# Scaling four PSUM banks behind the matmuls that fill their other halves, and keeping two SSM tables in their written order on VectorE

## The chip, the core and the metric

The kernel runs on one core of a Trainium2 chip. TensorE (PE in the profile, PEld its weight loads) multiplies and writes into eight PSUM banks of 128 partitions by 512 float32; VectorE (DVE), ScalarE (ACT) and GpSimd (POOL) do the element-wise work; the DMAs are all issued by SyncE's queue (SPq). The time is the device time of one execution in microseconds, and the number compared is the median of several executions.

## The reference, cut to what matters

One decoder layer on x of 512 tokens by 1024 features: a gated feed-forward network (FFN), a mixer of attention and a state space model (SSM), and a second FFN, each with an RMS norm ahead and behind.

```
h = x + 1/2 * post1(SwiGLU_1(pre1(x)))        # w_gate, w_up: 1024 x 2816, w_down: 2816 x 1024
u = pre_m(h);  [q | k | v | s] = u @ W_in
a = block-sparse causal attention(q, k, v);  z = GLU(S5 SSM over s)
h = h + post_m([rms(a) | rms(z)] @ W_out)
y = h + 1/2 * post2(SwiGLU_2(pre2(h)))
```

In the SSM every state decays by a complex factor a = exp(lam * dt). The kernel builds tables from lam, dt, b and c before the mixer needs them: the powers of one complex factor for 128 steps (the tiles `e0` and `e1`, real and imaginary part), and the input matrices (`si`, from the tiles `f` and `b`), besides two others. All are stored to DRAM and read again in the mixer.

## The kernel before, in words

All matrix products are done with operands split in two parts, a high one and a remainder (`w1`/`w2` of a weight, `xh`/`xl` or `sh`/`sl` of the activations), as three matmuls: high by high, high by remainder, remainder by high (L185, L186, L187). ScalarE makes the high parts, VectorE the remainders (L90/L91 and L274/L275 for weights, L463/L464 for the hidden rows).

**First FFN, start.** The input is transposed without its norm, since the norm of a token is one factor for a whole column. Four PSUM banks `gu_192` to `gu_195` hold gate and up products of the first two feature blocks; columns 0:256 are tokens 0 to 255, columns 256:512 the others. `first_half` fills the first halves with unnormalised activations. `halves` then fills the second halves, bank by bank, from activations that were normalised in time: 24 matmuls a bank. Behind the first of these banks comes `late_norm`: a matmul spreads the norms of tokens 0 to 255 over all partitions (L171), ScalarE copies the result into `rsb` (L173), VectorE and ScalarE scale and split the activations of these tokens (L177 to L179), and VectorE multiplies the first halves of the four banks by `rsb` (L181). Then feature blocks 2 to 7 follow in full width (banks `pg`, `pu`, 48 matmuls a block), and between their evacuations VectorE computes pieces of the SSM tables (`Tables.steps`, as many as `STEPS` says).

**First FFN, middle and end.** The feature blocks 8 to 21 are done in pairs with fewer products (L396), and then comes the down projection: 22 groups of 24 matmuls (L185 to L187, tile `d`), one for each block of the hidden rows, whose parts `sh` and `sl` sit in three rotating buffers. At each group one piece of `Tables.rest` is taken from a generator:

```
            for _ in range({0: 4, 1: 2}.get(i, 1)):
                next(self.filler or iter(()), None)
```

Its pieces are first eight steps of the powers (each a `cmul`, six VectorE instructions, L547 to L552, which doubles the powers known so far, at most 32 at once), then the eight stores of `e0` and `e1` (L721), then for each of four quarters the loads of `f` and `b` (L727, L728), one `cmul` into `st`, and two stores of `si` (L733). When eleven groups are done, `open_third` gives back the memory of the hidden rows of the second half and of the tables; the hidden parts and weights of the remaining eleven groups are put there, so these wait for the table's stores.

**What sets the order.** TensorE and GpSimd run in the order in which the program is written. On VectorE, ScalarE and SyncE a scheduler picks, at build time, from what its own timing holds ready; instructions under `high_priority` are picked first. Instructions wait for each other by tile regions and, in a PSUM bank, also where a matmul writes one half while another engine touches the other half. A marked instruction (`keep_in_program_order`) is kept behind the one written just before it on its engine.

Of the kernel before, what the change touches and what calls it, by code (L numbers as in the profile page):

```python
# [11 lines left out]
OP = mybir.AluOpType  # L12
# [3 lines left out]
P = 128  # L16
# [6 lines left out]
H = 256  # L23


class Core:
    def __init__(self, tc, ctx):
        self.tc = tc
        self.nc = nc = tc.nc
        self.ctx = ctx  # L30
        self.const = ctx.enter_context(tc.tile_pool(name="const", bufs=1))
        self.ps = ctx.enter_context(tc.tile_pool(name="ps", bufs=8, space=PSUM))
        self.wk = ctx.enter_context(tc.tile_pool(name="wk", bufs=1))
        self.wp = ctx.enter_context(tc.tile_pool(name="wp", bufs=4))
        self.identg = self.const.tile([P, P + NK], F32, name="ident")
        self.ident, self.gcol = self.identg[:, :P], self.identg[:, P:]
        self.h = [self.const.tile([P, D], F32, name=f"h{t}") for t in range(4)]
        self.xh = self.const.tile([P, NK, S], F32R, name="xh")
        self.xl = self.const.tile([P, NK, S], F32R, name="xl")
        self.mhalf = self.const.tile([P, 1], F32, name="mhalf")  # L40
        nc.vector.memset(self.mhalf, -0.5)
        self.n = 0
        self.xf = None
# [120 lines left out]
    def late_norm(self, banks):  # L164


        nc = self.nc
        v = nc.vector
        diag = self.diag
        pb = banks[-1][:, H:]  # L170
        nc.tensor.matmul(pb, nc.const_aps.tensor(1.0, [P, P], F32), diag[:, :H], start=True, stop=True)  # L171
        rsb = self.t512("rsb")[:, :H]
        nc.scalar.activation(rsb, pb, AF.Copy)  # L173
        for q in range(2):
            k = slice(4 * q, 4 * q + 4)
            f = self.xf[0][:, k]
            v.tensor_tensor(f, f, rsb.unsqueeze(1).to_broadcast([P, 4, H]), OP.mult)  # L177
            nc.scalar.activation(self.xh[:, k, :H], f, AF.Copy)
            v.tensor_tensor(self.xl[:, k, :H], f, self.xh[:, k, :H].bitcast(F32), OP.subtract)  # L179
        for b in banks:  # L180
            v.tensor_tensor(b[:, :H], b[:, :H], rsb, OP.mult)  # L181

    def mm3(self, out, ah, al, bh, bl, first, last):
        nc = self.nc
# [22 lines left out]
    def halves(self, units, hooks, begun=False):  # L207

        for half in range(begun, 2):
            for i, (u, pb) in enumerate(units):
                self.proj_T(u, pb, (half * H, half * H + H))
                if half == 0:
                    for f in hooks.get(i, ()):
                        f()
                if begun and i == 0:
                    with self.tc.high_priority(PRIO):
                        self.late_norm([pb for u, pb in units])

    def open_ffn(self, ctx, tab):

        def pool(name, c, bufs=1):
            self.n += 1
            return c.enter_context(self.tc.tile_pool(name=f"{name}_{self.n}", bufs=bufs, reuse_waits="tile"))
        self.hid = pool("hida", ctx)
        below, low, self.top = ExitStack(), ExitStack(), ExitStack()  # L230
        self.xsum = pool("xsum", below)
        self.filler = None
        if tab is not None:
            self.filler = tab.steps(pool("tab", self.top), self.nc.vector)

        def drain():
            for _ in self.filler or ():
                pass
            self.filler = None
            self.top.close()  # L240
            self.top = ExitStack()

        def first():
            drain()
            self.late = pool("hidb", low).tile([P, NF - HALF_F, S], F32, name=f"late_{self.n}")
            self.sum = pool("sum", self.top)

        def second():
            drain()
            p = pool("split", self.top, 3)  # L250
            if tab is not None:
                self.filler = tab.rest(pool("rest", self.top), self.xsum, self.nc.vector)
            return p

        def third():
            drain()
            low.close()
            below.close()
            return pool("last", self.top, LAST)
        self.open_first, self.open_second, self.open_third = first, second, third  # L260

    def ring(self, tag, n, dt):
# [263 lines left out]
PRIO = 400  # L526
# [18 lines left out]
def cmul(eng, ore, oim, ar, ai, br, bi, t1, t2):  # L545

    eng.tensor_tensor(t1, ar, br, OP.mult)  # L547
    eng.tensor_tensor(t2, ai, bi, OP.mult)
    eng.tensor_tensor(ore, t1, t2, OP.subtract)
    eng.tensor_tensor(t1, ar, bi, OP.mult)  # L550
    eng.tensor_tensor(t2, ai, br, OP.mult)
    eng.tensor_tensor(oim, t1, t2, OP.add)  # L552


class Tables:


# [140 lines left out]
    def rest(self, pool, wide, vec):  # L698


        nc, core = self.nc, self.core
        tt = wide.tile([P, 2, 512], F32, tag="t4", name="ett")
        tt = [tt[:, j] for j in range(2)]
        et = [wide.tile([P, 16, P], F32, tag=f"t{j + 1}", name=f"e{j}") for j in range(2)]
        vec.tensor_copy(et[0][:, :, 0], self.u4r)
        vec.tensor_copy(et[1][:, :, 0], self.u4i)
        n = 1
        while n < P:
            for lo in range(0, n, 32):
                m = min(32, n - lo)  # L710
                s1, s2 = (t[:, :16 * m].rearrange("p (c x) -> p c x", c=16) for t in tt)
                with core.tc.high_priority(PRIO):
                    cmul(vec, et[0][:, :, n + lo:n + lo + m], et[1][:, :, n + lo:n + lo + m],
                         et[0][:, :, lo:lo + m], et[1][:, :, lo:lo + m],
                         et[0][:, :, n - 1:n].to_broadcast([P, 16, m]), et[1][:, :, n - 1:n].to_broadcast([P, 16, m]),
                         s1, s2)
                yield
            n *= 2
        for q in range(4):
            for j in range(2):  # L720
                nc.sync.dma_start(self.e[j][q].rearrange("p (c x) -> p c x", c=4), et[j][:, 4 * q:4 * q + 4])  # L721
        for q in range(4):
            f, b = ([pool.tile([P, 512], F32, tag=f"{n}{j}", name=f"{n}{j}_{q}") for j in range(2)] for n in "fb")
            c = slice(512 * q, 512 * q + 512)
            for j in range(2):
                for s in range(4):
                    nc.sync.dma_start(f[j][32 * s:32 * s + 32], self.w[j, s:s + 1, c].partition_broadcast(32))  # L727
                nc.sync.dma_start(b[j], self.bturn[j, :, c])  # L728
            t = [pool.tile([P, 512], F32, tag=f"st{j}", name=f"st{j}_{q}") for j in range(2)]
            st = [core.t512("st") for j in range(2)]  # L730
            cmul(vec, *st, *f, *b, *t)
            for j in range(2):
                nc.sync.dma_start(self.si[j][q], st[j])  # L733
            yield
# [519 lines left out]
```

## Time and profile before

| | |
|---|---|
| median of 3 runs | 941.51 us (940.51 to 941.88) |
| profiled execution | 942.61 us, its span 940.6 us |
| mean granted TensorE clock | 0.989 of full speed |
| busy: PE, PEld, DVE, ACT | 98%, 88%, 73%, 45% of the span |
| TensorE waits of 1 us or more, each with its longest | gu on VectorE 5.4 us; sc on VectorE 2.4; d on ScalarE 2.4; d on VectorE 1.9 |

A row of the timeline has the start in microseconds from the span's start, the busy time, engine, line, operation, output and inputs with their shape, the count, and in brackets how long the engine was idle before and what ended that. A row of the windows has for each engine its busy time and instructions, then the granted TensorE clock (1.00 is 2.4 GHz, 0.50 is 1.2 GHz), the share of the DMA engines and their GB/s. In a row of waits stand the total, how often, and the longest.

### The profile page before, as it was taken

The page shows a single profiled execution, that of the slowest core. Times are in us where ns is not written, and L with a number is a line of the kernel's source. Part 1 is how long each engine was busy: PE and PEld are TensorE (multiplying, and loading weights), DVE is VectorE, ACT ScalarE, POOL GpSimd, SP SyncE. Part 2 cuts the span into 40 slices and gives each one's busy share as a digit, 9 for nine tenths or more (in the row PEclk, how much of TensorE's full clock was granted, in tenths as well). Part 3 has the DMA queues.
Part 4 walks back from the last instruction along what each step waited for, and adds up shares of the span by engine and source line. Part 5 has one row for each costly group of instructions (what it writes and reads, how often), then busy time and mean ns, then how long its engine had stood idle before and what let it go on. Part 6 is the DMA issues. An engine that isn't in the chain of part 4 may idle for free.

```text
span 940.6 us, 14870 instructions
## 1 busy us (share of the span) xinstructions
PE 918.6 (98%) x5815; PEld 824.7 (88%) x5815; DVE 689.0 (73%) x1179; ACT 427.8 (45%) x717; POOL 54.8 (6%) x47
## 2 busy tenths in 40 slices
PE   9799999999999899998999999999999999999997
PEld 8788899999988688987888778989999999988885
DVE  7997678888588655579999969698878887532623
ACT  7522345455422343333478866445445545422511
POOL 1400000000000001021120113000000000000000
PEclk9899999999999899999999999999999999999999
DMA  8436322322665561485432122322333323333302
GB/s 265 128 114 213 115 91 90 112 91 68 191 207 173 193 221 34 151 246 163 131 107 99 32 104 67 136 68 92 115 109 94 109 93 111 112 98 104 135 1 89
DMA packets 51574, 114.59 MB, mean 122 GB/s; under 512 B 9904, under 2 KB 20912, under 8 KB 51504
## 3 DMA queue, kind: packets, MB, share of 16 engines
q1 hardware_dynamic: 51504, 113.65, 37.5%
q8 instruction: 45, 0.74, 0.3%
q14 instruction: 25, 0.20, 0.1%
HBM read 102.62 MB, written 11.01 MB: 121 GB/s over the span
## 4 chain that ended last, share of the span: by engine, by line
PE 81%; DVE 8%; DMA 5%; ACT 2%; SPq 2%; issue 2%; POOL 0%; DVEq 0%; POOLq 0%; ACTq 0%
PE c L396 28%; PE d L187 6%; PE d L186 6%; PE d L185 6%; PE p L396 5%; DMA b<-in_bturn 2%; PE pg L185 2%; PE pg L187 2%; PE pu L187 2%; PE pu L185 2%; PE pg L186 2%; PE pu L186 2%; PE wo L187 1%; PE wo L185 1%; PE wo L186 1%
## 5 line engine op out<-in xcount | busy, mean ns | idle before, releaser
L396 PE MATMUL c<-xh,w 128*128 128x256 f32 x1024 | 187.2, 281 | 0.1
L396 PEld LDWEIGHTS c<-xh,w 128*128 128x128 f32 x1024 | 159.3, 189 | 0.3 <-DVE w L275 0.3
L90 ACT ACTIVATE w<-w 128x1024 fp32r<-128x1024 f32 x90 | 94.3, 1055 | 108.9 <-PE d L187 22.5
L396 PE MATMUL c<-xl,w 128*128 128x256 f32 x512 | 143.8, 281 | 0.0
L91 DVE TENSOR_TENSOR w<-w,w 128x1024 fp32r<-128x1024 f32 x90 | 111.3, 1243 | 41.2 <-ACT w L90 41.0
L185 PE MATMUL d<-w,sh 128*128 128x512 f32 x352 | 138.2, 393 | 2.4 <-ACT sh L463 2.4
L187 PE MATMUL d<-w,sl 128*128 128x512 f32 x352 | 138.1, 392 | 1.9 <-DVE sl L464 1.9
L275 DVE TENSOR_TENSOR w<-w,w 128x1024 fp32r<-128x1024 f32 x96 | 116.9, 1222 | 29.4 <-ACT w L274 28.8
L186 PE MATMUL d<-w,sh 128*128 128x512 f32 x352 | 137.9, 392 | 0.0
L274 ACT ACTIVATE w<-w 128x1024 fp32r<-128x1024 f32 x96 | 100.2, 1058 | 72.5 <-PE c L396 45.3
L396 PE MATMUL c<-t,w 128*128 128x256 f32 x768 | 97.4, 283 | 0.1
L396 PEld LDWEIGHTS c<-xl,w 128*128 128x128 f32 x512 | 96.6, 189 | 0.0
L396 PEld LDWEIGHTS c<-t,w 128*128 128x128 f32 x768 | 94.3, 191 | 0.3 <-DVE w L275 0.3
L185 PEld LDWEIGHTS d<-w,sh 128*128 128x128 f32 x352 | 66.7, 189 | 16.7 <-ACT sh L463 2.8
L187 PEld LDWEIGHTS d<-w,sl 128*128 128x128 f32 x352 | 66.7, 190 | 16.2 <-DVE sl L464 2.3
L186 PEld LDWEIGHTS d<-w,sh 128*128 128x128 f32 x352 | 66.7, 189 | 13.7
L61 POOL TENSOR_TENSOR rs<-v,mhalf 128x1 f32<-128x1 f32 x24 | 20.0, 835 | 733.6 <-DVE v L57 733.6
L396 PE MATMUL p<-t,s1h 128*128 128x256 f32 x256 | 46.5, 282 | 0.0
L463 ACT ACTIVATE sh<-late 128x512 fp32r<-128x512 f32 x22 | 13.4, 630 | 60.9 <-PE d L186 60.9
L456 ACT ACTIVATE sg<-c 128x256 f32<-128x256 f32 x64 | 24.5, 382 | 33.6 <-DVE c L414 26.8
L396 PEld LDWEIGHTS p<-t,s1h 128*128 128x128 f32 x256 | 39.7, 190 | 0.0
L396 PE MATMUL p<-t,s1l 128*128 128x256 f32 x128 | 36.1, 282 | 0.0
(318 smaller groups left out, 1768.8 us busy)
## 6 DMA issues: line engine op xcount, KB each, us to landing
w<-in_wgu SPq DMA_DIRECT2D x88, 512.0 KB, 3.6
w<-in_wd SPq DMA_DIRECT2D x44, 512.0 KB, 3.9
e<-e SPq DMA_DIRECT2D x16, 256.0 KB, 4.4
w<-in_wq SPq DMA_DIRECT2D x8, 512.0 KB, 3.8
g<-in_gains SPq DMA_DIRECT2D x5, 512.0 KB, 5.4
h<-in_x SPq DMA_DIRECT2D x4, 512.0 KB, 6.1
ca<-cx SPq DMA_DIRECT2D x8, 256.0 KB, 2.9
f<-win SPq DMA_DIRECT2D x32, 64.0 KB, 3.2
```

Of the source, the lines that this page charges most:

```text
L61: self.nc.gpsimd.tensor_tensor(rs, v, self.mhalf, OP.pow)
L90: nc.scalar.activation(hi, raw, AF.Copy)
L91: (eng or nc.vector).tensor_tensor(lo, raw, hi.bitcast(F32), OP.subtract)
L185: nc.tensor.matmul(out, ah, bh, start=first, stop=False)
L186: nc.tensor.matmul(out, ah, bl, start=False, stop=False)
L187: nc.tensor.matmul(out, al, bh, start=False, stop=last)
L274: nc.scalar.activation(hi, src, AF.Copy)
L275: nc.vector.tensor_tensor(lo, src, hi.bitcast(F32), OP.subtract)
L396: nc.tensor.matmul(out, l[:, s], r[:, kb + k, t], start=first and k == 0 and n == 0, stop=last and k == 3 and n == 2, skip_group_check=True)
L456: nc.scalar.activation(sg, pg, AF.Silu)
L463: nc.scalar.activation(hi, hidden[k], AF.Copy)
```

## The change

Two things are edited. The four multiplications of the banks leave `late_norm`; they are written behind the loop of `halves` and without high priority, so behind all second halves. And the powers lose their high priority; all VectorE instructions of `Tables.rest` (powers and inputs' table) now go through a small wrapper that keeps each behind the instruction written before it on VectorE. No operation is added or removed. (The rows of these instructions have the wrapper's line, L563, in the new kernel; other lines move down by 1 to 11.)

```
@@ late_norm
-        for b in banks:
-            v.tensor_tensor(b[:, :H], b[:, :H], rsb, OP.mult)
+        self.rsb = rsb
@@ halves
                 if begun and i == 0:
                     with self.tc.high_priority(PRIO):
                         self.late_norm([pb for u, pb in units])
+        for u, pb in units if begun else ():
+            self.nc.vector.tensor_tensor(pb[:, :H], pb[:, :H], self.rsb, OP.mult)
@@ open_ffn
-                self.filler = tab.rest(pool("rest", self.top), self.xsum, self.nc.vector)
+                self.filler = tab.rest(pool("rest", self.top), self.xsum, InOrder(self.tc, self.nc.vector))
+class InOrder:
+    def __init__(self, tc, eng):
+        self.tc, self.eng = tc, eng
+    def __getattr__(self, name):
+        return lambda *a, **k: self.tc.keep_in_program_order(getattr(self.eng, name)(*a, **k))
@@ rest
-                with core.tc.high_priority(PRIO):
-                    cmul(vec, ...)
+                cmul(vec, ...)
```

TensorE's and GpSimd's orders stay as they were. On the other engines rows move in three places.

**VectorE behind `late_norm`.** `gu` are the four banks, `xf` and `xl` the activations of tokens 0 to 255 and their remainders, `w_45` the weights of the second product of block 2. Before:

```order
L177 TENSOR_TENSOR xf_106<-xf_106,rsb_396 128x1024 x2
L181 TENSOR_TENSOR gu_192<-gu_192,rsb_396 128x256
L181 TENSOR_TENSOR gu_193<-gu_193,rsb_396 128x256
L181 TENSOR_TENSOR gu_194<-gu_194,rsb_396 128x256
L181 TENSOR_TENSOR gu_195<-gu_195,rsb_396 128x256
L604 SCALAR_TENSOR_TENSOR ssm_small<-ssm_small 128x16
L299 TENSOR_TENSOR xf_107<-xf_107,xf_106 128x1024
L582 TENSOR_TENSOR ssm_small<-ssm_small 128x16
L179 TENSOR_TENSOR xl<-xf_106,xh 128x4x256 x2
```

and now:

```order
L177 TENSOR_TENSOR xf_106<-xf_106,rsb_396 128x1024 x2
L220 TENSOR_TENSOR gu_192<-gu_192,rsb_396 128x256
L615 SCALAR_TENSOR_TENSOR ssm_small<-ssm_small 128x16
L220 TENSOR_TENSOR gu_193<-gu_193,rsb_396 128x256
L300 TENSOR_TENSOR xf_107<-xf_107,xf_106 128x1024
L593 TENSOR_TENSOR ssm_small<-ssm_small 128x16
L91 TENSOR_TENSOR w_45_572<-w_44_569,w_45_571 128x1024
L179 TENSOR_TENSOR xl<-xf_106,xh 128x4x256
L615 SCALAR_TENSOR_TENSOR ssm_small<-ssm_small 128x16
L220 TENSOR_TENSOR gu_194<-gu_194,rsb_396 128x256
L179 TENSOR_TENSOR xl<-xf_106,xh 128x4x256
```

The four scalings are spread, the last stands further down, behind what is shown, and a weight's remainder has come ahead of the two rows that make `xl`.

**VectorE near the end of the tables**, groups 8 to 11 of the down projection. `e_2848` and `e_2849` are the powers, `ett` their scratch, `st` the inputs' table. Before:

```order
L464 TENSOR_TENSOR sl_3319<-late_1031,sh_3318 128x512
L91 TENSOR_TENSOR w_327_3366<-w_326_3363,w_327_3365 128x1024
L549 TENSOR_TENSOR e_2848<-ett 128x16x32
L550 TENSOR_TENSOR ett<-e_2848,e_2849 128x512
L551 TENSOR_TENSOR ett<-e_2849,e_2848 128x512
L552 TENSOR_TENSOR e_2849<-ett 128x16x32
L91 TENSOR_TENSOR w_329_3400<-w_328_3397,w_329_3399 128x1024
```

and now:

```order
L563 TENSOR_TENSOR e_2848<-ett 128x16x32
L563 TENSOR_TENSOR st_3_3238<-f_3_3224,b_3_3226 128x512
L563 TENSOR_TENSOR ett<-e_2848,e_2849 128x512
L563 TENSOR_TENSOR ett<-e_2849,e_2848 128x512
L465 TENSOR_TENSOR sl_3319<-late_1031,sh_3318 128x512
L91 TENSOR_TENSOR w_327_3366<-w_326_3363,w_327_3365 128x1024
L563 TENSOR_TENSOR st_3_3239<-f_3_3225,b_3_3227 128x512
L563 TENSOR_TENSOR e_2849<-ett 128x16x32
L563 TENSOR_TENSOR st_3240<-st_3_3238,st_3_3239 128x512
```

The last write of `e_2848` has moved ahead of the remainders `sl_3319` and `w_327`, and the fourth quarter of the inputs' table, which stood ahead of it all before, is now partly behind the last write of `e_2849`.

**SyncE's queue at the same place.** `e_97` and `e_98` are the powers in DRAM, `w_330` and `w_332` raw weights. Before:

```order
L80 DMA w_330_3431<-in_wd 128x1024
L733 DMA si_94<-st_3241 128x512
L80 DMA w_332_3465<-in_wd 128x1024
L721 DMA e_97<-e_2848 128x512 x4
L721 DMA e_98<-e_2849 128x512 x4
L80 DMA w_334_3499<-in_wd 128x1024
```

and now:

```order
L80 DMA w_330_3431<-in_wd 128x1024
L730 DMA e_97<-e_2848 128x512 x4
L80 DMA w_332_3465<-in_wd 128x1024
L730 DMA e_98<-e_2849 128x512 x4
L742 DMA si_93<-st_3240 128x512
L80 DMA w_334_3499<-in_wd 128x1024
L742 DMA si_94<-st_3241 128x512
```

The first four stores of the powers have moved ahead of the load of `w_332`, and the last two stores of the inputs' table have moved behind the powers' stores.

More of the change, by code (lines that the diff above doesn't have):

```diff
@@ L711, in rest @@
                 s1, s2 = (t[:, :16 * m].rearrange("p (c x) -> p c x", c=16) for t in tt)
-                with core.tc.high_priority(PRIO):
[L713 to L716, printed above, removed]
+                cmul(vec, et[0][:, :, n + lo:n + lo + m], et[1][:, :, n + lo:n + lo + m],
+                     et[0][:, :, lo:lo + m], et[1][:, :, lo:lo + m],
+                     et[0][:, :, n - 1:n].to_broadcast([P, 16, m]), et[1][:, :, n - 1:n].to_broadcast([P, 16, m]), s1, s2)
                 yield
```

## The prediction

> **What bounds the kernel now.** I read first the busy times, then TensorE's waits, then the windows and the timeline around each wait. TensorE is busy 98% of the span, so only two things can shorten it: its waits, and stretches in which it runs at half clock.
>
> ```profile
> PE 918.6 (98%) x5815; PEld 824.7 (88%) x5815; DVE 689.0 (73%) x1179; ACT 427.8 (45%) x717; POOL 54.8 (6%) x47
> ```
>
> The list of TensorE's waits has four of a microsecond or more that the profile names once each:
>
> ```profile
> PE gu L185 <- DVE gu L181: 5.4, 1, 5.4
> PE sc L841 <- DVE y L942: 2.4, 1, 2.4
> PE d L185 <- ACT sh L463: 2.4, 1, 2.4
> PE d L187 <- DVE sl L464: 1.9, 1, 1.9
> ```
>
> The first stands in the stretch of the late scaling, the last two are one stop in the first down projection; the second belongs to the mixer, where the change moves nothing. The windows show that the first costs more than its wait:
>
> ```profile
> 27.00:32.30 5.30, 0.00 (x0) 0.00 (x0) 5.26 (x14) 2.12 (x4) 4.55 (x2) 0.69 0.36 120
> 32.30:36.00 3.70, 3.70 (x17) 3.70 (x18) 3.70 (x7) 3.19 (x4) 2.08 (x1) 0.52 0.79 256
> 36.00:40.00 4.00, 4.00 (x36) 4.00 (x35) 4.00 (x9) 1.45 (x2) 0.00 (x0) 1.00 0.02 4
> 112.00:200.00 88.00, 88.00 (x742) 88.00 (x741) 67.99 (x101) 43.51 (x71) 0.00 (x0) 1.00 0.30 99
> ```
>
> TensorE does nothing from 27.0 to 32.3, its clock falls to the lower level, 17 matmuls run at half speed, and only then is the clock full. In the 88 us of the pairs that follow it never stops while VectorE has 20 us to spare: what is won ahead of them is kept.
>
> **Term 1: the banks.** The timeline of TensorE (first four rows) and of VectorE around the wait:
>
> ```profile
> 26.25 0.70 PE L171 MATMUL gu<-diag,const-float32-1.0 128*128 128x256 f32 x2 [0.15 <-DVE diag L1218]
> 32.30 0.58 PE L185 MATMUL gu<-xh,first 128*128 128x256 f32 x1 [5.35 <-DVE gu L181]
> 36.12 0.28 PE L185 MATMUL gu<-xh,first 128*128 128x256 f32 x1
> 42.51 0.40 PE L185 MATMUL pg<-xh,w 128*128 128x512 f32 x1
> 29.22 2.35 DVE L177 TENSOR_TENSOR xf<-xf,rsb 128x1024 f32<-128x1024 f32 x2
> 31.49 1.42 DVE L181 TENSOR_TENSOR gu<-gu,rsb 128x256 f32<-128x256 f32 x4
> 32.91 1.23 DVE L299 TENSOR_TENSOR xf<-xf,xf 128x1024 f32<-128x1024 f32 x1
> 34.15 2.36 DVE L179 TENSOR_TENSOR xl<-xf,xh 128x1024 fp32r<-128x1024 f32 x2
> ```
>
> The matmul at 32.30 opens the second bank's second half, and waits until VectorE has scaled its first half, since that scaling was written ahead of it. Its operands were ready long before. In the change the 72 matmuls of banks two to four follow the norm matmul at once. That at 36.12 is the 19th, and the 54 from it to the first `pg` took 42.51 - 36.12 = 6.39 us, 0.118 each; so 72 take 8.52 us and `pg` could issue at 26.95 + 8.52 = 35.47 instead of 42.51: 7.04 us, of them 5.35 the wait and the rest the half clock.
>
> The next thing that can be late is `xl`, which the second `pg` matmul reads. In the new order VectorE does, from 31.49: two scalings (2 x 0.36), two small rows (0.2), L299 (1.23), a weight's remainder that has come ahead (1.22) and the first half of `xl` (1.18): 36.0 at most, 35.85 with the usual overlap of 0.1 a row. That matmul would issue at 35.7. I take 0.3 us of waiting; below it is 0, above it is 1.9, if the matmul waits for both halves of `xl` (one more scaling and 1.18 us, to 37.6). The short waits of 0.9 us at 9 us cost no clock, since the windows there are at 1.00:
>
> ```profile
> 0.00:10.00 10.00, 8.05 (x49) 6.21 (x49) 5.60 (x15) 6.29 (x12) 0.20 (x4) 1.00 0.80 295
> ```
>
> The scalings cost the same four times 0.36 us on VectorE. Now each waits for TensorE to leave its bank: the second bank at 26.95 + 2.84 = 29.8, the third at 32.6, the fourth at 35.5. VectorE reaches them at 31.9, 35.9 and about 40 (behind `xl`, a gain of 0.7, an evacuation of 0.7 and a weight of 1.2), so it waits for none. The Trainium skill speaks against cheap hopes here: "PSUM — Partial Sum Buffer", section "PSUM bank collisions raise a hardware error", says that two engines must not touch one bank at the same partitions at once, whichever columns; by it no scaling can run beside its bank's matmuls, and the sum is the same, as they are reached later anyway. The old 5.35 us between disjoint halves of a bank agree with it.
>
> What comes after on this side is the matmuls with table entries, which TensorE reaches 6.7 us earlier:
>
> ```profile
> 76.98 0.69 DVE L670 TENSOR_TENSOR cx<-tt,tt 128x512 f32<-128x512 f32 x1
> 87.30 0.27 PE L677 MATMUL si<-ident,win 128*128 128x128 f32 x1
> ```
>
> The third update of `cx` by L670 is the last these need; it ended at 77.7. In the new order two more weight remainders, two scalings and half of `xl` lie ahead of it and one weight less behind 36 us (2 x 1.22 + 0.72 + 1.18 - 1.22 = 3.1, less 0.6 that the queue starts earlier): 80.2 at most, against 80.6. Nothing, with 0.4 us to spare; the upper bound is 1 us. Behind them SyncE's queue has changed too:
>
> ```profile
> 80.75 5.50 SPq L694 DMA_DIRECT2D ca<-cx  x8
> 98.60 0.69 DVE L351 TENSOR_TENSOR h<-w 128x512 f32<-128x512 f32 x1 [1.08 <-DMA w<-in_wgu]
> 112.36 0.28 PE L396 MATMUL c<-xh,w 128*128 128x256 f32 x1
> ```
>
> The eight `ca` stores now leave behind the last `cx`, and the load that VectorE got at 98.6 waits for them. Even 7 us later, at 105.6, with two VectorE rows and one of ScalarE (2.0) on top, its sums are there at 107.6; TensorE wants them 36 matmuls of 0.118 into the pairs, at 112.36 + 4.2 - 6.7 = 109.9. No cost. Term 1 is 7.04 - 0.3 = **6.7 us**.
>
> **Term 2: the tables.** TensorE at the stop, the chain of waits (the row without a line number), and the two engines and the queue behind it:
>
> ```profile
> 304.79 0.39 PE L186 MATMUL d<-w,sh 128*128 128x512 f32 x1
> 311.82 0.39 PE L187 MATMUL d<-w,sl 128*128 128x512 f32 x1
> 314.61 0.50 PE L185 MATMUL d<-w,sh 128*128 128x512 f32 x1 [2.40 <-ACT sh L463]
> 317.23 0.79 PE L187 MATMUL d<-w,sl 128*128 128x512 f32 x1 [1.88 <-DVE sl L464]
> 322.79 0.39 PE L185 MATMUL d<-w,sh 128*128 128x512 f32 x1
> 313.93 0.63 ACT L463 ACTIVATE sh<-h 128x512 fp32r<-128x512 f32 x1 [6.06 <-DMA e<-e]
> 316.48 2.54 DVE L464 TENSOR_TENSOR sl<-h,sh 128x512 fp32r<-128x512 f32 x4 [4.83 <-DMA e<-e]
> 312.04 4.32 DMA e<-e
> 307.35 5.46 SPq L721 DMA_DIRECT2D e<-e  x8
> 308.68 0.69 DVE L552 TENSOR_TENSOR e<-ett 128x512 f32<-128x512 f32 x1
> 297.13 0.69 DVE L548 TENSOR_TENSOR st<-f,b 128x512 f32<-128x512 f32 x1 [3.00 <-DMA b<-in_bturn]
> ```
>
> The 32 matmuls from 304.79 to 311.82 are 0.227 apart. The one at 322.79 is the 16th of the twelfth group and would have come at 311.82 + 16 x 0.227 = 315.45: the stop costs 7.34 us, 4.28 waiting and 3.06 at half clock. Its cause: the memory of this group's parts holds the powers until all eight stores have left; these are issued in one row of 5.46 us from 307.35, the last at 312.04, which lands at 316.36.
>
> In the new order four rows of the inputs' table (the end of its fourth quarter, 4 x 0.69 = 2.8) stand behind the last write of the powers and no longer ahead of it. The wait of 3.00 for the load of `b` stood ahead too; the row that waits for that load now has a hidden row's remainder (0.69) and a weight's (1.22) and powers' rows ahead that used to be behind it. So the last write ends, in the time of before, at 309.37 - 2.8 = 306.6 at the latest, and at 309.37 - 2.8 - 3.0 = 303.6 if the load is covered, as I take it. The first four stores go out earlier, when `e0` is done, so four remain: three issues of 0.68 (5.46 / 8) and a landing of 4.32 after the last begins: 309.9, or 312.9 at the bound. The remainder then takes VectorE 0.69, and TensorE wants it at 312.05 + 0.45 = 312.5. At 309.9 there is no stop, 1.9 us to spare; at the bound it is 1.1 us late. So this term lies between 7.34 - 1.1 - 3.06 = 3.2 (late and clock lost) and 7.34; I take **7.3**, being nearer the first by the covered load. The remainders of groups 4 to 11 cost nothing either: adding up the rows of the new order, with the loads of `b` at the median below, each ends 2 to 6 us earlier than before against TensorE. The inputs' table is stored last at about 305, as before; the mixer's first load of it is at 380:
>
> ```profile
> b<-in_bturn SPq DMA_DIRECT2D x8, 256.0 KB, 4.5
> 304.89 0.69 DVE L464 TENSOR_TENSOR sl<-late,sh 128x512 fp32r<-128x512 f32 x1
> 380.30 0.80 SPq L893 DMA_DIRECT2D si<-si  x2
> ```
>
> **Sum.** 6.7 + 7.3 = 14.0 us. Against the profiled execution of 942.6 us this is 928.6; the median of the runs shown is 1.1 lower, so 927.5.
>
> **The rivals.**
> (A) Both stops go, as summed: 927.5.
> (B) The second stop stays in part: a load of `b` that lands late delays the last write. For it speaks the 3.00 us of before, against it that only one of six such waits was over 1.5 us:
>
> ```profile
> DVE st L548 <- DMA b<-in_bturn: 3.9, 2, 3.0
> DVE st L547 <- DMA b<-in_bturn: 3.6, 3, 1.5
> DVE st L548 <- DMA f<-win: 1.1, 1, 1.1
> ```
>
> Between 927.5 + 1.1 and, with the whole stop, 927.5 + 7.3: near 932.
> (C) The first stop turns into smaller ones, 1.6 more at `xl` or 1 at the table's matmuls, with up to 1.7 of half clock: 929 to 931.
> (D) Slower. VectorE works off its queue in order; with the table's rows held behind their predecessors, a row that waits for a load holds up the remainders behind it, as in those 3.0 us. TensorE notices once such waits together pass the lead of the remainders, some 6 us (that of group 11 was done at 305.6, can now be done near 303.6 - 0.69 - 0.69 - 1.22 = 301, and is used at 307). It decides once what is lost beyond that lead passes the 14.0 us of the sum; if the six rows wait 4 us longer each it is 24 us, 18 beyond the lead, and three stops with 3.06 of half clock each, so 27 us on top of 927.5: 954. Against it: those waits were 8.6 us in all. The Trainium skill has the rule in "PSUM — Partial Sum Buffer", section "Engine vs sequencer instructions": VectorE's queue is strictly first in, first out. By it a late load is paid in full by all that stands behind; the trace agrees with the 3.0 us.
> (E) The change does not do what it says: if TensorE also waited at 27 us for ScalarE or the activations, the stop would stay. The row of the wait names L181 alone. With the tables' stop kept as well, 941.5.
>
> **How the numbers follow.** A 70%, B 14%, C 9%, D 4%, E 3%. The range holds A with its unknown costs, C and the nearer part of B: from 925.5 (the 0.3 us at `xl` not paid and up to 1.7 of the mixer's 2.4 us gone) to 934.0. Faster by over 0.2%, which is about what a measurement of this kernel can tell from no change, are A, B and C: 0.93. Within it E: 0.03. Slower D: 0.04.
>
> **What would show it.** Right: no wait of `gu` for L220 at 27 us, windows from 27 to 40 at clock 1.00, `pg` at 35.5 to 36; the first `si` matmul near 80.6; no `d` wait for `sh` or `sl`, the last store of the powers issued before TensorE's group 11 ends, and clock 1.00 throughout the down projection. Wrong: a `pg` wait for `xl` of over 2 us, an `m` wait for `cx`, or `d` still waiting for the powers' stores, or for `sl` with VectorE held by a load of `b`.

## The result, and the profile after

The changed kernel takes 928.54 us (median of 4 runs, 927.66 to 929.68), the kernel before 941.69 us beside it (4 runs, 940.51 to 944.28). The ratio is 0.9843, with a 95% interval of 0.9822 to 0.9865; of 941.69 us that is 12.7 to 16.8 us saved. The two medians alone lie 13.15 us apart, inside that interval. In a second comparison the ratio was 0.9845 (0.9824 to 0.9866). The profiled execution took 929.68 us with a span of 927.9 (before 942.61 and 940.6). Forecast were 927.5 us and 14.0 saved.

The busy times, and three rows of the list of TensorE's waits, in the profile of the changed kernel:

```profile
PE 914.2 (99%) x5815; PEld 821.7 (89%) x5815; DVE 689.1 (74%) x1179; ACT 427.0 (46%) x717; POOL 54.9 (6%) x47
```

```profile
PE sc L850 <- DVE y L951: 2.6, 1, 2.6
PE gu L171 <- DVE diag L1227: 0.8, 1, 0.8
PE pg L185 <- DVE xl L179: 0.2, 1, 0.2
```

The wait of 5.4 us of `gu` for the scaled banks is gone, and so are both waits of `d` (2.4 and 1.9). The mixer's wait of `sc` stands as it stood. In place of the first wait there is one of 0.2 for `xl`. The windows of the two stretches (columns as in the prediction: window, its length, busy time of TensorE, weight loads, VectorE, ScalarE, GpSimd, then the granted clock, the DMA share and GB/s):

```profile
27.00:36.00 9.00, 8.76 (x72) 8.71 (x73) 8.96 (x19) 6.07 (x8) 6.96 (x3) 1.00 0.55 189
36.00:40.00 4.00, 3.79 (x18) 2.93 (x18) 4.00 (x8) 2.90 (x4) 0.00 (x0) 1.00 0.61 207
305.00:320.00 15.00, 15.00 (x67) 12.28 (x66) 10.44 (x13) 9.35 (x13) 0.00 (x0) 1.00 0.53 189
```

The stretch from 27 to 32.3 held no matmul before, and the one behind it ran at clock 0.52. Now TensorE works through, at 1.00. The timelines of TensorE and of VectorE there:

```profile
27.24 0.70 PE L171 MATMUL gu<-diag,const-float32-1.0 128*128 128x256 f32 x2 [0.79 <-DVE diag L1227]
27.58 0.47 PE L184 MATMUL gu<-xh,first 128*128 128x256 f32 x1
36.30 0.39 PE L184 MATMUL pg<-xh,w 128*128 128x512 f32 x1
36.89 0.50 PE L185 MATMUL pg<-xl,w 128*128 128x512 f32 x1 [0.21 <-DVE xl L179]
```

```profile
32.49 0.41 DVE L220 TENSOR_TENSOR gu<-gu,rsb 128x256 f32<-128x256 f32 x1
32.93 0.41 DVE L220 TENSOR_TENSOR gu<-gu,rsb 128x256 f32<-128x256 f32 x1
35.63 1.21 DVE L179 TENSOR_TENSOR xl<-xf,xh 128x1024 fp32r<-128x1024 f32 x1
36.88 0.41 DVE L220 TENSOR_TENSOR gu<-gu,rsb 128x256 f32<-128x256 f32 x1
40.76 0.41 DVE L220 TENSOR_TENSOR gu<-gu,rsb 128x256 f32<-128x256 f32 x1
```

The second bank follows the norm matmul after 0.34 us; before, it followed after 6.05. This execution is 0.99 us later than that of before at the norm matmul (27.24 against 26.25), so 0.99 is to be taken off its times when they are set against the forecast's. The scalings of banks two to four then stand at 31.9, 35.9 and 39.8.

In the down projection, VectorE, SyncE's queue, ScalarE, and TensorE's twelfth group:

```profile
297.72 0.68 DVE L563 TENSOR_TENSOR e<-ett 128x512 f32<-128x512 f32 x1
305.95 2.54 DVE L465 TENSOR_TENSOR sl<-h,sh 128x512 fp32r<-128x512 f32 x4 [2.55 <-DMA e<-e]
294.08 2.68 SPq L730 DMA_DIRECT2D e<-e  x4
298.43 2.21 SPq L730 DMA_DIRECT2D e<-e  x4
302.04 0.61 ACT L464 ACTIVATE sh<-h 128x512 fp32r<-128x512 f32 x1
306.77 0.43 PE L186 MATMUL d<-w,sl 128*128 128x512 f32 x1
```

The last write of the powers starts at 297.72, 51.3 us behind the first `d` matmul (246.45); before it was 56.5 (308.68 against 252.18). The stores leave in two rows of four. VectorE still waits 2.55 us for the last of them, but TensorE hardly does: the matmul at 306.77, the first that needs the remainder, starts on its turn of 0.227 us, and the next one comes 0.04 us behind its own.

**By stages.** Three marks on TensorE's timeline cut the program: the norm matmul, the first and the last `d` matmul of the first down projection. "Left" is from there to the last matmul. The numbers are differences of start times, in us. The rows that are neither before nor changed are kernels of the experiments below.

| kernel, profiled execution | norm matmul at | norm to first `pg` | norm to first `d` | first to last `d` | left |
|---|---|---|---|---|---|
| before | 26.25 | 16.26 | 225.93 | 128.61 | 553.22 |
| before, again | 26.08 | 16.60 | 226.27 | 126.68 | 553.46 |
| changed | 27.24 | 9.06 | 219.21 | 121.37 | 553.44 |
| changed, again | 27.19 | 8.95 | 219.26 | 121.26 | 553.77 |
| late scaling alone | 26.68 | 9.06 | 219.20 | 125.38 | 553.45 |
| late scaling alone, again | 27.24 | 9.06 | 219.19 | 123.27 | 553.50 |
| written order alone | 26.90 | 16.83 | 226.51 | 121.82 | 553.78 |
| without the last loads of `b` | 26.66 | 16.04 | 225.71 | 125.34 | 553.68 |
| wait filled with matmuls | 26.95 | 14.67 | 224.39 | 128.86 | 555.35 |
| wait filled, again | 26.39 | 14.74 | 224.41 | 127.60 | 555.53 |
| last write later, 2 rows | 26.25 | 8.95 | 219.24 | 121.26 | 553.46 |
| last write later, 6 rows | 27.41 | 9.05 | 219.20 | 129.44 | 553.43 |
| sign change later | 25.62 | 8.95 | 219.26 | 121.32 | 553.71 |
| one more bank taken | 27.16 | 9.48 | 219.29 | 121.32 | 553.13 |

From before to changed the second column of stages gives 225.93 - 219.21 = 6.72 us, the third 128.61 - 121.37 = 7.24, the start takes 0.99 and the rest 0.22: 12.75, against 12.7 of the spans.

### The profile page after: what moved, and what is told of

Same layout as the page of the kernel before. It is cut to its first block, busy times and chain, and to the rows that moved or that the text cites. A ratio compares the mean times of both kernels' runs of the same rounds, so it can differ in the third digit from the quotient of the medians.

```text
span 927.9 us, 14869 instructions
## 1 busy us (share of the span) xinstructions
PE 914.2 (99%) x5815; PEld 821.7 (89%) x5815; DVE 689.1 (74%) x1179; ACT 427.0 (46%) x717; POOL 54.9 (6%) x47
## 4 chain that ended last, share of the span: by engine, by line
PE 87%; DVE 5%; DMA 4%; ACT 2%; issue 1%; SPq 1%; DVEq 0%; POOLq 0%; ACTq 0%
PE c L397 29%; PE d L184 9%; PE d L186 9%; PE d L185 9%; PE p L397 5%; PE pg L185 2%; PE pu L185 2%; PE pg L186 2%; PE pu L186 2%; PE pu L184 2%; PE pg L184 2%; PE wo L186 1%; PE wo L184 1%; PE wo L185 1%; DMA h<-in_x 1%
```

## The experiments

**Each part alone.** The first kernel is before with the scaling moved, the second before with the wrapper and without the priority:

```diff
 late scaling alone, in late_norm and behind the loop of halves:
-        for b in banks:
-            v.tensor_tensor(b[:, :H], b[:, :H], rsb, OP.mult)
+        self.rsb = rsb
...
+        for u, pb in units if begun else ():
+            self.nc.vector.tensor_tensor(pb[:, :H], pb[:, :H], self.rsb, OP.mult)
 written order alone:
-                self.filler = tab.rest(pool("rest", self.top), self.xsum, self.nc.vector)
+                self.filler = tab.rest(pool("rest", self.top), self.xsum, InOrder(self.tc, self.nc.vector))
...
-                with core.tc.high_priority(PRIO):
```

> Only the scaling of the banks' first halves is moved; the tables keep the order of before. Theory (the two gains are separate, the first is 5.35 us of waiting and 1.7 us of half clock less a wait for xl): 941.7 - 6.7 = 935.0 us, no gu wait for L220, clock 1.00 from 27 to 40 us, and the stop of the down projection unchanged at 2.4 + 1.9 us of waiting. Rival 1 (TensorE would have waited there for something else): 940 to 942. Rival 2 (the two parts lean on each other, since VectorE is then late somewhere behind): 931 or 938 and a stop of another length.

> Only the powers and the inputs' table keep their written order; the scalings stand where they stood before. Theory (the whole stop of 4.28 us and its 3.06 us of half clock go): 941.7 - 7.3 = 934.4 us, no d wait for sh or sl. If the last store lands as late against TensorE as in the changed kernel, where the remainder came with nothing to spare, the wait is between 0 and 0.3 us. Rival (the stop goes only because TensorE's times were shifted by the first part): a d wait of 1 us or more stays and the time is 936 to 940.

Late scaling alone took 932.72 us (4 runs) against 944.36 of before, ratio 0.9878 (0.9863 to 0.9893), so 10.1 to 12.9 us; expected were 6.7. Written order alone took 936.52 (5 runs), ratio 0.992 (0.9908 to 0.9933): 6.3 to 8.7 us, expected 7.3. Both at once gave 0.9845. The parts therefore do not add: alone they are worth 0.0202 together, at once 0.0155. For late scaling alone the theory (935.0 us) missed, and the second rival's 931 us is nearer: the two parts do lean on each other. The waits of TensorE, first of the kernel with late scaling, then of that with the written order:

```profile
PE d L186 <- DVE sl L465: 1.9, 1, 1.9
PE pg L185 <- DVE xl L179: 0.2, 1, 0.2
```

```profile
PE gu L185 <- DVE gu L181: 5.4, 1, 5.4
PE d L187 <- DVE sl L464: 0.2, 1, 0.2
```

Each does to its own stop what the theory says. But late scaling alone also took away the wait for `sh` and left only 1.9 of the 4.3 us. The stage table shows the same: 219.20 as in the changed kernel, and then 125.38 instead of 128.61.

Of the second part the wrapper does all: with the priority alone dropped, all engines have exactly the order of before, and with the wrapper and the priority kept that of the wrapper alone.

**Was that chance?** The same two kernels once more, word for word, for a second profiled execution:

> The kernel before once more, for a second profiled execution: the second stage, from the first to the last d matmul of this projection, took 128.6 us in the first. Theory 1 (the length of the stop differs from execution to execution with the landing of the loads of f and b, and the first part's kernel met a short one by chance): it is 1 us or more off, as low as 126. Theory 2 (it is the same every time, and the late scaling really shortens it to 125.4): 128 to 129 again.

> The kernel with the late scaling alone once more: its stage from the first norm matmul to the first d matmul took 219.2 us as in the changed kernel, but the next one 125.4 instead of 128.6, and the ratio was 0.988 where the sum says 0.993. Theory 1 (chance in the landing of loads): the stage takes 126 to 129 us this time and the time comes nearer the 0.993. Theory 2 (the late scaling shortens the stop as well): 125.4 and 0.988 again.

Before took 941.88 us in its one run, with a stage of 126.68 from the first to the last `d`, so the stop is not the same each time. Late scaling alone took 931.6 us (5 runs) against 943.62, ratio 0.9879 (0.9862 to 0.9895), with a stage of 123.27. So both theories hold a part: the length differs by 2 us between executions of one kernel, and below that late scaling does shorten it, by (128.61 + 126.68 - 125.38 - 123.27) / 2 = 3.3 us. Two executions each are few; but the two of the kernel with added matmuls further down, 128.86 and 127.60, lie with before. What carries it is the last long wait of VectorE for a load, and the last write (before again, then late scaling again):

```profile
296.51 0.69 DVE L548 TENSOR_TENSOR st<-f,b 128x512 f32<-128x512 f32 x1 [3.17 <-DMA b<-in_bturn]
308.06 0.69 DVE L552 TENSOR_TENSOR e<-ett 128x512 f32<-128x512 f32 x1
```

```profile
288.56 0.69 DVE L549 TENSOR_TENSOR st<-f,b 128x512 f32<-128x512 f32 x1 [2.35 <-DMA b<-in_bturn]
300.11 0.69 DVE L553 TENSOR_TENSOR e<-ett 128x512 f32<-128x512 f32 x1
```

Counted from the first `d` matmul (252.35 and 246.43) the row behind the load stands at 44.2 and 42.1, and the last write at 55.7 and 53.7. The order of VectorE, ScalarE and SyncE is the same in both kernels all through this stage; their differences end ahead of it. Set against each other row by row, the two come apart at rows of `st` that wait (0.3, 0.7 and 0.8 us at three of them, 0.2 at the others; where the profile names what ended such a wait it is a load), and the 2.0 us that add up so reach the last write undiminished. Why the loads land sooner when TensorE and the queues come to this stage 7 us earlier is open. In the written order it makes little difference: the stage takes 121.82 without late scaling and 121.37 and 121.26 with it, since a wait of 0.2 us is all of the stop that is left to shorten.

**What of the second stop is the load.** Before, without the two loads of `b` for the last quarter:

```diff
-            f, b = ([pool.tile([P, 512], F32, tag=f"{n}{j}", name=f"{n}{j}_{q}") for j in range(2)] for n in "fb")
+            f = [pool.tile([P, 512], F32, tag=f"f{j}", name=f"f{j}_{q}") for j in range(2)]
+            if q < 3:
+                b = [pool.tile([P, 512], F32, tag=f"b{j}", name=f"b{j}_{q}") for j in range(2)]
...
-                nc.sync.dma_start(b[j], self.bturn[j, :, c])
+                if q < 3:
+                    nc.sync.dma_start(b[j], self.bturn[j, :, c])
```

> The kernel before without the two loads of b for the last quarter of the inputs' table (that quarter is computed from the third quarter's b, so the last quarter of that table is not the reference's). Theory (3.0 us of the stop in the down projection are VectorE standing before that load with the powers' rows queued behind it): the wait of 3.0 goes, the last write of the powers is 2.5 to 3.0 us earlier against TensorE, the stop shrinks from 4.3 to 1.3 us, and the time by 3 to 6 us, with half clock: 936 to 939. Rival (VectorE waits as long for the f load or something else in the same place): no change, 941.7.

It took 939.63 us (10 runs, 935.76 to 942.67) against 944.18, ratio 0.995 (0.9931 to 0.9969): 2.9 to 6.5 us less. The last write and TensorE's stop:

```profile
306.34 0.69 DVE L552 TENSOR_TENSOR e<-ett 128x512 f32<-128x512 f32 x1
314.97 0.50 PE L187 MATMUL d<-w,sl 128*128 128x512 f32 x1 [1.97 <-DVE sl L464]
```

The write is 54.0 us behind the first `d` (252.37) instead of 56.5 or 55.7, and the wait is 1.97 instead of 4.28. So the rows of powers did stand behind that load, and TensorE paid for it. The run understates this: in this execution VectorE also waited 2.84 us for an early load of `b`, against 0.88 and 1.16 in the two of before, and its rows were 0.9 and 1.7 us later than theirs against TensorE before it came to the place. How the 2.0 us of wait that are left divide between that and the other rows ahead of the last write was not separated.

**How much is to spare in the changed kernel.** In its profile the remainder came just in time, where the prediction had 1.9 us to spare. Two kernels compute the last product of the powers again (2 and 6 times), ahead of the last write:

```diff
-def cmul(eng, ore, oim, ar, ai, br, bi, t1, t2):
+def cmul(eng, ore, oim, ar, ai, br, bi, t1, t2, again=0):
...
-    eng.tensor_tensor(t2, ai, br, OP.mult)
+    for _ in range(1 + again):
+        eng.tensor_tensor(t2, ai, br, OP.mult)
     eng.tensor_tensor(oim, t1, t2, OP.add)
...
+                     again=2 if n + lo == P - 32 else 0)
```

> The changed kernel with the last product of the powers computed three times over in place of once, 2 rows of 0.6 us more ahead of the last write; with three rows of the inputs' table and the rows that pass it, the write comes about 3.0 us later. By the prediction (the last store lands 1.9 us before TensorE needs the remainder): a d wait for sl of 1.1 us. By the trace of the changed kernel (nothing to spare, TensorE waited 0.04 us): a wait of 3.0 us. Half clock behind it 0 to 3 us. So 929.6 against 931.5 to 934.6.

> As the run with 2 rows, with 6: together with four rows of the table and two remainders that pass it, the last write comes about 8.3 us later. By the prediction's margin of 1.9 us a d wait of 6.4 us, by the trace of the changed kernel one of 8.3 us, and 3 us of half clock behind either: 938 against 940. If the wait of TensorE does not grow with the lateness of the write, the powers' stores are not what it waits for.

> The changed kernel once more, beside a kernel that moves only the sign change and three others on the same chip. By stages, from the first norm matmul to the first d matmul 219.2 us (225.9 before) and from there to the last d matmul of this projection 121.4 (128.6 before); the rest within 0.5 us of before, so that the two stages carry the whole difference. If the sign change is worth 1 us, this one is 1 us above that kernel's ratio of 0.9845.

With 2 rows: 928.65 us (4 runs), ratio 0.9848, the same as the changed kernel beside it (929.03, 0.9845). With 6 rows: 938.48 us, ratio 0.9944 (0.9923 to 0.9965). The last write, the remainder and (where there are any) TensorE's waits, of 2 rows, and then of 6:

```profile
298.25 0.68 DVE L564 TENSOR_TENSOR e<-ett 128x512 f32<-128x512 f32 x1
303.80 2.54 DVE L465 TENSOR_TENSOR sl<-h,sh 128x512 fp32r<-128x512 f32 x4 [1.37 <-DMA e<-e]
```

```profile
305.20 0.68 DVE L564 TENSOR_TENSOR e<-ett 128x512 f32<-128x512 f32 x1
312.22 1.94 DVE L465 TENSOR_TENSOR sl<-h,sh 128x512 fp32r<-128x512 f32 x3 [3.23 <-DMA e<-e]
308.31 0.50 PE L184 MATMUL d<-w,sh 128*128 128x512 f32 x1 [1.67 <-ACT sh L464]
312.96 0.80 PE L186 MATMUL d<-w,sl 128*128 128x512 f32 x1 [3.93 <-DVE sl L465]
```

And of the changed kernel's second profiled execution, the remainder and the matmul that needs it:

```profile
297.46 0.68 DVE L563 TENSOR_TENSOR e<-ett 128x512 f32<-128x512 f32 x1
304.44 2.54 DVE L465 TENSOR_TENSOR sl<-h,sh 128x512 fp32r<-128x512 f32 x4 [1.05 <-DMA e<-e]
306.77 0.39 PE L186 MATMUL d<-w,sl 128*128 128x512 f32 x1
```

From the first `d` (246.45, 245.49 and 246.61) the last write of these three starts at 51.0, 52.8 and 58.6. The 2 rows only cost it 1.75 us, not 3.0, since VectorE's waits ahead of it were shorter in this execution (3.2 us in sum against 4.5), and TensorE did not wait at all: neither forecast for this kernel came. The 6 rows cost 7.6, and TensorE waited 1.67 + 3.93 = 5.6 us: 2.0 us of the delay were free (1.7 against the first execution, whose last write started at 51.3, but whose stores landed later). The first of the two waits is not the stores' doing: in this kernel ScalarE's order has one more weight ahead of `sh`, which waits for TensorE until 306.68, when the four stores of `e0` had long landed. It adds no waiting of its own, since the matmul that reads `sl` starts at 312.96 either way, 6.0 us behind its turn. The second execution shows the same directly: the first of the four remainders ends at about 304.44 + 0.63 = 305.1, and is needed at 306.8, 1.7 us to spare. By the same count the first profile had 0.2 (305.95 + 0.63 against 306.77), since its stores landed later. The wait of TensorE grows with the write's delay beyond that margin, and VectorE's remainder waits 3.23 us for the landing of `e`: the powers' stores are what TensorE waits for.

**The clock's share of the first stop.** Before with 44 matmuls into a bank of their own, behind the norm matmul:

```diff
         nc.scalar.activation(rsb, pb, AF.Copy)
+        spare = self.bank("spare")
+        for n in range(44):
+            k = n % NK
+            nc.tensor.matmul(spare[:, :H], unit[0][:, k * P:(k + 1) * P], self.xh[:, k, H:2 * H],
+                             start=n == 0, stop=n == 43)
```

> The kernel before with 44 matmuls of 128x256 whose result nothing reads, put behind the norm matmul into the stretch in which TensorE waited for the scalings. Theory (1.7 of the first term's 7.04 us is the lower clock after the wait): the wait is filled, the clock stays at 1.00 through 40 us, the second halves run 0.118 us apart from the first, and pg comes at 40.8 instead of 42.5: 941.7 - 1.7 = 940.0. Rival 1 (the lower clock has no part in it, the matmuls would have run as slowly for another reason): 941.7 with 0.21 us between them. Rival 2 (the added matmuls disturb the scalings next to them in PSUM): the wait grows and the time is above 942.

> The kernel with the added matmuls once more: it reached pg 1.6 us earlier against the norm matmul, as expected, but its time was that of before (ratio 1.0002, 0.9992 to 1.0012). If the 1.6 us are lost in the later stop, the stage from the first to the last d matmul takes 130 us, 1.5 more than in the kernel before; if they were lost by chance in the single waits that its profile shows elsewhere (1.4 of c for a weight, 1.1 of gu for the diagonal), the time is now 1 to 2 us below before, ratio 0.998 to 0.999.

TensorE's timeline and the windows of the first of the two:

```profile
26.95 0.70 PE L171 MATMUL gu<-diag,const-float32-1.0 128*128 128x256 f32 x2 [1.10 <-DVE diag L1223]
27.29 5.55 PE L177 MATMUL spare<-xh,first 128*128 128x256 f32 x44
33.00 0.38 PE L190 MATMUL gu<-xh,first 128*128 128x256 f32 x1 [0.15 <-DVE gu L186]
41.62 0.40 PE L190 MATMUL pg<-xh,w 128*128 128x512 f32 x1
```

```profile
27.00:32.30 5.30, 5.30 (x43) 5.25 (x44) 5.26 (x12) 1.45 (x2) 3.86 (x2) 1.00 0.31 104
32.30:36.00 3.70, 3.55 (x30) 3.34 (x29) 3.70 (x8) 3.67 (x4) 2.78 (x1) 1.00 0.82 291
```

The clock stays at 1.00, the 72 matmuls of the three banks take 41.62 - 33.00 = 8.62 us instead of 42.51 - 32.30 = 10.21, and the first `pg` comes 14.67 us behind the norm matmul instead of 16.26: 1.6 us, as the theory has it. The time, however, did not follow: ratios 1.0002 (0.9992 to 1.0012) and 1.0006 (0.9995 to 1.0016). The stage table tells where it went: not into the stop (128.86 and 127.60, as in before), but into "left", 555.4 and 555.5 instead of 553.1 to 553.8, both times. The one wait of over 1 us that is new there:

```profile
PE c L401 <- DVE w L280: 1.4, 1, 1.4
```

It lies in the second FFN, far behind the edit, and makes up 1.2 to 1.4 of the 1.9 to 2.1 us; where the rest is lost, in the mixer, was not followed up. The extra bank moves about half of the later PSUM tiles to another bank, so I took that for the cause and tried it alone, in the changed kernel:

```diff
         nc.scalar.activation(rsb, pb, AF.Copy)
+        nc.tensor.matmul(self.bank("spare")[:, :H], nc.const_aps.tensor(1.0, [P, P], F32), diag[:, :H], start=True, stop=True)
```

> The changed kernel with one more PSUM bank taken once (a copy of the norm matmul into it, 0.1 us, which nothing reads), so that every later tile of PSUM gets the next bank in turn. Theory (the kernel with 44 added matmuls paid its 1.6 us back because its extra bank shifted all the later ones: in both its executions the stage from the first pg of the second layer's feed-forward to its first d matmul took 204.6 us instead of 203.4, with a c wait of 1.4 for a weight, and the stage from sc to wo 0.8 more): 204.6 again, the c wait of 1.4 is there, and 928.7 + 2 = 930.7. Rival (the shifted banks are not the cause, the moved rows of the other engines near the added matmuls are): 203.4, no c wait, 928.8.

929.63 us (4 runs), ratio 0.9856 (0.9833 to 0.9878), "left" 553.13 and no such wait. The theory of the shifted banks fell, at least in this kernel. Moved rows cannot bring it directly either: the orders of VectorE, ScalarE and SyncE differ from those of before only in the first FFN, far ahead of the wait. What the traces show is one load of a weight. It is issued 30.5 us behind the second FFN's first `pg` in every execution, and lands after 4.7 us in both with added matmuls, after 3.3 to 3.6 in the 12 others. Why it does is open.

**A version with the sign change out of the way.** In the changed kernel `diag`, which the norm matmul needs, stands on VectorE behind the sign change of a part of `cx`, which waits for its load (2.36 us in the profile). One line holds it further back:

```diff
-        vec.tensor_scalar(cx[1][:, :, 0], cx[1][:, :, 0], -1.0, None, op0=OP.mult)
+        core.tc.keep_in_program_order(
+            vec.tensor_scalar(cx[1][:, :, 0], cx[1][:, :, 0], -1.0, None, op0=OP.mult))
```

> The changed kernel, with the sign change of cx held behind the product that precedes it in the code, so that it no longer stands ahead of the diagonal on VectorE, waiting for its load. Theory (in the changed kernel this row holds VectorE for 2.36 us, of which TensorE pays the 0.8 us that gu waits for the diagonal and the 0.2 that pg waits for xl): both waits go and the time is 928.5 - 1.0 = 927.5. Rival 1 (TensorE is then held by ScalarE's or GpSimd's part of the norm): 928.5. Rival 2 (the sign change, now later, makes the third cx late for the matmuls that read it, which had 0.7 us to spare): an m wait of 0.5 us or more, 928.5 to 929.5.

VectorE's second `diag`, and the norm matmul:

```profile
23.77 0.29 DVE L1228 TENSOR_SCALAR diag<-ident,rs 128x128 f32<-128x128 f32 x1 [0.24 <-POOL rs L61]
25.62 0.59 PE L171 MATMUL gu<-diag,const-float32-1.0 128*128 128x256 f32 x2
```

The wait of `gu` for the diagonal went, and no wait for `cx` came; the norm matmul is the earliest of all profiles. But it took 929.29 us (4 runs), ratio 0.9845 (0.9831 to 0.9859), the same ratio as the changed kernel. A gain of up to 1 us is inside the interval and cannot be told from none. The wait it takes away is not there each time: in the changed kernel's second profile it was below 0.2. I leave the changed kernel as the best version.

## Why the prediction came out as it did

**The first term (6.7 us, the banks)** measured 6.72 in the profiles, and 225.7 to 226.5 against 219.2 to 219.3 in all. That it fits to 0.02 us is luck, two small misses of opposite sign: up to `pg` 7.20 us were won instead of 7.04 (16.26 less 9.06), and 0.48 instead of 0.3 were lost behind it, most of it at `xl`, where the second `pg` matmul started 0.59 us behind the first instead of 0.23. Its steps held too. `pg` was to come 9.22 us behind the norm matmul and came at 9.06; the new wait for `xl` was put at 0.3 and was 0.2 (0.4 in the second execution). The scalings were placed at 31.9, 35.9 and about 40 and stood at 31.9, 35.9 and 39.8, none waiting. The third `cx` row was allowed 80.2 and the matmuls with table entries 80.6; counted from the same start they came at 80.22 + 0.69 - 0.99 = 79.9 and 81.57 - 0.99 = 80.58, so 0.7 was to spare. The clock's 1.7 in the sum is 1.6 in the run with added matmuls, where it shows alone. The 5.35 us of before do not test by themselves whether two engines may touch one bank at once, as the prediction has it: that wait is one that the program sets, and in the changed kernel every scaling comes after TensorE has left its bank.

**The second term (7.3 us, the tables)** measured 7.24 between the first profiled executions, with one of which it was made; so close a hit is luck of the pair, since against the second execution of before it is 5.4. The mechanism is shown: without the load of `b` the write comes 2.5 us earlier, and with the write held back TensorE waits again once 1.7 to 2.0 us are used up; the forecast had 1.9. The last write was put at 303.6, 51.4 behind the first `d`, and ended at 52.0 and 51.7. The single landing of 4.32 after the last issue was a weak guess: the last store landed after 6.0 in the first execution, 5.9 with the written order alone, 4.7 in the second execution and 3.4 with 2 rows. In the first that used up most of the margin without costing anything.

**What the prediction had wrong** is a step it took without saying so: that the second stop has one length, and that the first part leaves it as it is. The stop costs 7.3 us in one execution of before and 5.4 in another (128.61 and 126.68 less 121.3), and 2.0 to 4.1 with late scaling alone. For the pair this does not matter, since the written order takes away whatever is left. For a part alone it does: late scaling alone was forecast to save 6.7 us and saved 4 to 5 us more. The saving also depends on the executions of before that are compared: its medians were 941.7 to 944.4 us in the five comparisons, and the changed kernel's lay 13.15 us below in the first and 15.15 in the second, around the forecast 14.0. Where the slower executions of before lose their time is not shown, since both profiled ones (942.6 and 941.9) are among the faster.

**The rest**: the forecast of 927.5 was 1.0 below the measured median, and the profiled pair differ from its sum by 0.99 at the norm matmul, ahead of everything that the change touches; in the 14 profiles this point lies between 25.6 and 27.4. The rivals: (B), the second stop staying in part, came near in the first profile (0.2 us to spare) and was not paid; of (C) there is only the 0.2 at `xl`; (E) fell with the wait of 5.4 us; (D), late loads held up in VectorE's order, did not show: VectorE waits at most 2.1 us in one row of the table, and TensorE's lead covers it. The Trainium skill's "PSUM — Partial Sum Buffer", section "Engine vs sequencer instructions", has VectorE's queue strictly first in, first out; the traces agree: without the load of `b` that held VectorE for 3.0 us, the last write behind it is 2.5 us earlier (1.7 against the second execution of before).

## What to carry to other kernels

When an engine in the middle works off one queue for two customers, look for what its rows are queued behind, not only for what they wait for: here four scalings and four table rows were moved, none removed, and 13 to 15 us came free. The stop that ended with a DMA landing had no fixed length here, so take two profiled executions before pricing its parts, and cut the program at marks on the bounding engine: stages that agree to a few tenths between executions show at once where a change acts and what only drifts. A gain at one place is booked only when the stages behind it keep their length.

## What the runs showed of the hardware

The powers' stores of 256 KB each landed after 4.3 to 5.1 us when eight left in one row (4.0 to 4.7 in the second execution of before), and after 5.5 to 6.0 in the changed kernel (4.2 to 6.6 in its second execution), although the last four had a row of their own. The windows of that stretch show the DMA engines busy throughout (a packet counts in full where it starts, so that a share can be above 1):

```profile
298.40:300.70 2.30, 2.30 (x12) 1.91 (x11) 2.27 (x5) 0.00 (x0) 0.00 (x0) 1.00 1.06 407
300.70:306.00 5.30, 5.30 (x25) 4.40 (x24) 2.64 (x4) 1.65 (x3) 0.00 (x0) 1.00 1.03 389
```

The landings go with that share only roughly. From the first issue of the last four to the last landing it was 1.04, 1.02 and 1.03 where these four took 5.5 to 6.0 (changed), 5.9 to 6.4 (written order alone) and 4.2 to 4.7 us (changed, again), 0.94 where they took 4.3 to 4.8 (6 rows later), and 0.90 where they took 2.8 to 3.4 (2 rows later). What sets them beyond that was not tested. The other surprise is how well TensorE's stages repeat: what is left behind the first down projection, some 553 us, lies between 553.1 and 553.8 in 12 of the 14 executions, on several chips, while whole runs of one kernel differ by 2 us or more.

The price of a stop beyond its waiting goes with the granted clock behind it. Against 121.3 us without a stop, the waits of 5.6, 4.3, 3.2, 2.0, 1.9 and 1.7 us (6 rows later; before; before again; without `b`; late scaling, and again) made the stage 8.1, 7.3, 5.4, 4.0, 4.1 and 2.0 us longer, so beyond the waiting 2.5, 3.0, 2.2, 2.1, 2.2 and 0.3 were lost. The mean granted clock of 20 us around the stop (from 305 in the kernels with late scaling, from 310 in the others) was 0.83, 0.83, 0.91, 0.91, 0.91 and 1.00 in the same order. The last two are the same kernel: in one execution the clock fell behind a wait of 1.9 us, in the other it stayed full behind one of 1.7.

```profile
305.00:320.00 15.00, 13.09 (x49) 10.05 (x49) 8.62 (x11) 7.35 (x11) 0.00 (x0) 0.89 0.49 160
305.00:320.00 15.00, 13.29 (x59) 10.69 (x58) 8.81 (x12) 8.21 (x13) 0.00 (x0) 1.00 0.58 196
```

So part of what set these executions of one kernel apart is whether a short stop brought the lower clock with it.
